# A transformer-like encoder layer on one core: the sums of the second MLP product's weights, made earlier and with GpSimd's own transfers

## The chip, the cores and the metric

The kernel runs on one core of a Trainium2 chip. A core has TensorE (matmuls; in the profile PE, with PEld for its weight loads), VectorE (DVE), ScalarE (ACT), GpSimd (POOL) and SyncE (SP). Each engine works through its own list of instructions in order and waits on semaphores for the others; transfers between memory and the on-chip buffer are issued as instructions of one engine's list and then run on 16 shared DMA engines. The metric is the device time of one execution in microseconds (us), the median of the runs shown. An engine's list that holds transfers is called its queue here.

## The reference

One encoder layer on 2048 tokens of width 1024, all in float32:

```
h   = RMSNorm(x);  z, xbc, dt, q, k, v = split(h @ W_in)
y_s = state-space heads(xbc, dt, z)          # forward and backward scan in chunks of 128
y_a = windowed attention(q, k, v)            # 16 heads, blocks of 128 with both neighbours
x   = x + RMSNorm(concat(y_s, y_a) @ W_out)
x   = x + RMSNorm(relu(RMSNorm(x) @ W_up)^2 @ W_down)
```

W_up is 1024 x 4096, W_down 4096 x 1024.

## The kernel before

Every array lies in tiles of 128 partitions by 512 columns. A float32 product is made of three matmuls in a rounded format: each operand is split into a high and a low part (`ws[:, 0]` and `ws[:, 1]` for weights), and high x high, high x low and low x high are summed in PSUM.

The main program works in this order: the input projection for the second half of the tokens (k and v, then eight q products), then for the first half (dt and v, k, q, then the convolution inputs and z), with attention blocks in between from the point where the second half's q, k, v are stored; the scan; the output projection; the two MLP products. TensorE's order is fixed by hand: `drive` advances the main generator and the side generators by an estimate of TensorE's time. The order on the other engines comes from the compiler's scheduler, which may put an instruction well ahead of the place where the program writes it, as soon as its inputs and buffers allow it.

**Weights of the input projection.** `wchunk` (L215 to L226) loads a tile `wr` from SyncE's queue, makes the high part with one GpSimd instruction (L222) and the low part with another (L225). There are four `ws` buffers of which a product uses two, so a product's weights are made while the one before it runs. `fill_h` and `split_slot` (L205) make the low parts of the normed input `h`, every second one on GpSimd; L342 and L343 split the weights of dt and v there.

**The MLP products** follow a fast algorithm for 2 x 2 blocks with 7 products for 8 (numbered 1 to 7 in the code), in two halves `hf` and groups `p` of seven steps of 12 matmuls. Its operands are sums of blocks. For the first product, `up_weights` makes the sums of W_up's blocks as it goes (L964, L969, L970), `up_input` and `up_input1` those of the input; the latter reads the second half's copies `dxo` from memory (L199 `stg`, L1012, L1013). Results go out by `dop` stores (L1079). For the second product, `down_weights` reads the sums of W_down's blocks from the array `dws` in memory, which `sums` fills.

**`sums`** (L1145) is a side generator, started in the first half of the first MLP product after group 3. It does 20 jobs, one after the other: four for the second half of x (load four tiles L1158, scale them on VectorE L1167, four operations on GpSimd L1169 to L1172, seven stores L1185 to `dxo`), then sixteen for W_down (load four tiles L1160, four additions or subtractions on GpSimd L1179, four stores L1187 to `dws`). Its tiles `sum` come from a set of four buffers (`nt`) that the norms use too. All its transfers are in SyncE's queue.

Of the kernel before, what the change touches and what calls it, by code (L numbers as in the profile page):

```python
# [38 lines left out]
class Layer:  # L39
# [73 lines left out]
    def drive(self, main):  # L113
        cond, mt = None, 0.0
        alive = True
        while alive or self.sides:
            s = next((s for s in self.sides if s[1] <= self.t and self.ready(s[2])), None)
            if s is not None:
                self.step_side(s)
            elif alive and mt <= self.t and self.ready(cond):  # L120
                cond, mt = next(main, self), self.t
                if cond is self:
                    alive, cond = False, None
                elif isinstance(cond, (int, float)):
                    mt, cond = self.t + cond, None
            else:
                c = [s[1] for s in self.sides if self.ready(s[2])]
                if alive and self.ready(cond):
                    c.append(mt)
                assert c, "stuck"  # L130
                self.t = max(self.t, min(c))
# [490 lines left out]
    def ssd_fwd(self, pool):  # L622
# [52 lines left out]
        def gate(c, g, y, sz, sums):  # L675
            pt = self.ps("pst")
            for i in range(4):
                self.tr(pt[:, i * P:(i + 1) * P], y[:, i * P:(i + 1) * P])
            nc.vector.tensor_mul(sz, sz, pt.rearrange("p (j t) -> p j t", j=4))
            nc.sync.dma_start(self.d_g[4 * g:4 * g + 4, :, c * P:(c + 1) * P].rearrange("j p t -> p j t"), sz)  # L680
            sq = pool.tile([P, 4, P], F32, tag="yt", name="gsq", bufs=2)
            nc.scalar.activation(sq, sz, AF.Square)
            s = pool.tile([P, P], F32, tag="gsum", name="gsum")
            nc.vector.reduce_sum(s, sq.rearrange("p j t -> p t j"), axis=mybir.AxisListType.X)
            if g:
                nc.vector.tensor_add(s, s, sums[c])
                nc.sync.dma_start(self.d_gs[:, c * P:(c + 1) * P], s)
                self.flags.add(f"ssd{c}")
            sums[c] = s
# [20 lines left out]
        for u in range(2 * NCH):  # L710
            c, g = u // 2, u % 2
            t0, pace = self.t, "ssd_pace2" if "att" in self.flags else "ssd_pace"
            if g == 0 and c < NCH - 1:
                ldn = self.ssd_load(pool, c + 1)
            if last:
                yield self.until(f"z{last[0] // 8}")
                sz = load_z(*last[:2])
            y = pool.tile([P, 512], F32, tag="y", name="y")
            yield from off(c, g, ld, prep, pb, y)
            nxt = prep  # L720
            if g and c < NCH - 1:
                if c + 1 < NCH - 1:
                    pb = load_pb(c + 1)
                yield K["ssd_p"]
                nxt = self.ssd_prep(pool, c + 1 == NCH - 1, *ldn)
            yield max(K["ssd_y"], t0 + K[pace] * K["ssd_f1"] - self.t)
            yield from diag(g, Es, ld[0], y)
            if last:
                gate(*last, sz, sums)
            yield max(K["ssd_y"], t0 + K[pace] * K["ssd_f2"] - self.t)  # L730
            if u < 2 * NCH - 1:
                Es = yield from expo((u + 1) % 2, *nxt[:3])
            last = (c, g, y)
            if g and c < NCH - 1:
                ld, prep = ldn, nxt
            yield max(K["ssd_y"], t0 + K[pace] - self.t)
        sz = load_z(*last[:2])
        yield 4
        gate(*last, sz, sums)


# [400 lines left out]

        self.pend.append(fn)

    def sums(self):  # L1145


        nc = self.nc
        vec = self.vec["norm_mlp_pre"]

        def load(job):
            a = {}
            for i in range(2):
                for k in range(2):
                    t = a[f"{i + 1}{k + 1}"] = self.nt("sum")
                    if len(job) == 1:
                        kt = 4 * i + job[0]
                        nc.sync.dma_start(t, self.d_x2[kt, :, self.tok(1, k)])  # L1158
                    else:
                        nc.sync.dma_start(t.rearrange("p (k c) -> p k c", k=4),  # L1160
                                          self.a["w_down"][2 * job[1] + i, 2 * job[0] + k])
            return a

        def x_sums(i, a):
            for y in ("11", "12", "22", "21"):
                kt = 4 * int(y[0]) - 4 + i
                nc.vector.tensor_scalar(a[y], a[y], vec[:, kt:kt + 1], None, ALU.mult)  # L1167
            t1, t2, t4 = self.ld(name="t1"), self.gl("t2"), self.ld(name="t4")
            nc.gpsimd.tensor_sub(t1, a["12"], a["11"])  # L1169
            nc.gpsimd.tensor_sub(t2, a["22"], t1)  # L1170
            nc.gpsimd.tensor_sub(a["12"], a["22"], a["12"])
            nc.gpsimd.tensor_sub(t4, a["21"], t2)  # L1172
            return {1: a["11"], 3: a["22"], 2: a["21"], 5: t1, 6: t2, 7: a["12"], 4: t4}

        def w_sums(qt, p, a):
            r = {}
            for m, fn, x, y, o in ((5, "tensor_add", "21", "22", "21"), (6, "tensor_sub", "21", "11", "11"),
                                   (7, "tensor_sub", "22", "11", "22"), (3, "tensor_sub", "12", "11", "12")):
                getattr(nc.gpsimd, fn)(a[o], a[x], a[y])  # L1179
                r[m] = a[o]  # L1180
            return r

        def store(m, job, a):
            if len(job) == 1:
                nc.sync.dma_start(self.d_xo[m - 1, job[0]], a)  # L1185
            else:
                nc.sync.dma_start(self.d_ws[(5, 6, 7, 3).index(m), job[0], job[1]], a)  # L1187
        jobs = [(i,) for i in range(4)] + [(qt, p) for qt in range(4) for p in range(4)]
        for n, job in enumerate(jobs):
            a = load(job)  # L1190
            yield 10
            r = (x_sums if len(job) == 1 else w_sums)(*job, a)
            yield 8
            for m, t in r.items():
                store(m, job, t)
            if n == 3:
                self.flags.add("xo")
            elif n > 3 and job[1] == 3:
                self.flags.add(f"sum{job[0]}")
            yield 5  # L1200

# [205 lines left out]
    def main(self):  # L1407
        nc, a, tc = self.nc, self.a, self.tc
# [50 lines left out]
        yield from self.dtvk(pp, 0, h, w)  # L1459
        yield from self.proj_q(pp, 0, h)  # L1460
        self.flags.add("qkv0")
        for c, j in self.p1a():
            yield from (self.proj_xbc(pp, 0, h, j) if c == "x" else self.proj_z(0, h, j))

# [74 lines left out]
        for hf in range(2):  # L1539
            for p in range(16):  # L1540
                if (hf, p) == (1, 15):
                    ws = itertools.chain(ws, self.down_weights())
                if p == 8:
                    self.side(self.r2(hf))
                if p == 14:
                    self.side(self.down_input() if hf else self.up_input1(B[1]))
                yield from self.up(hf, p, B[hf], wsa)
                if hf == 0 and p == 3:
                    yield self.until("x2_10", "x2_11")
                    s3.close()  # L1550
                    self.side(self.sums())
        self.worder = [("w_down", j, (6, 7)) for j in range(8)]
        while self.pend:
            self.pend.pop(0)()
# [108 lines left out]
```

## Time and profile before

| | us |
|---|---|
| median of 3 runs | 3213.89 |
| lowest and highest | 3203.62, 3218.38 |
| the profiled execution | 3205.63 |
| its span, first to last instruction | 3203.8 |

The profile's page shows one execution: busy time of each engine, the DMA queues, the chain of work that ended last. The trace behind it can be asked for a stretch: what an engine did in order of time (a timeline; in brackets the idle time before an instruction and what ended it), who waited for whom, and busy times and granted clock by stretch. TensorE's clock has two levels, 1.2 and 2.4 GHz; a granted clock of 1.00 is the upper one all the time.

### The profile page before, as it was taken

Reading aid. Unit: us, or ns where it says so; the run is one execution under the profiler, and the core shown is the slowest. Engines: PE = TensorE matmul, PEld = TensorE weight load, DVE = VectorE, ACT = ScalarE, POOL = GpSimd, SP = SyncE. Lnnn points to the kernel's source line nnn. Section 1 sums busy time; section 2 is a strip of 40 time slices with the busy share of each in tenths; the row PEclk is TensorE's granted clock in tenths of the full one; section 3 lists DMA queues with packets and bytes.
Section 4 is the critical chain, followed back from the end, with each engine's and each line's share of the span. In section 5 each row is a group of like instructions: output and inputs, shape, how many; then the busy total and the mean of one; then the engine's idle time right before and its main releaser. Section 6 shows DMA issues by size and latency. Waiting matters only on the chain. (4 is left out here: it accounts for less than half of the span.)

```text
span 3203.8 us, 41029 instructions
## 1 busy us (share of the span) xinstructions
PE 2949.0 (92%) x13560; PEld 2358.2 (74%) x13560; DVE 2196.2 (69%) x3671; ACT 1554.0 (49%) x2886; POOL 903.7 (28%) x743
## 2 busy tenths in 40 slices
PE   7989999989999899898897878998998999998996
PEld 6778887878886576576575657776887888877886
DVE  7355555547756778867868867677767567776765
ACT  4234566567765545322223354656565644454432
POOL 4242222112224344555545522141203000020001
PEclk9999999999999999899898989999999999999998
DMA  6767544465567755556436458778647565557633
GB/s 228 238 205 198 155 130 119 122 203 156 138 192 241 238 143 163 164 181 187 119 101 221 165 189 274 243 257 279 239 165 271 193 207 192 189 188 222 229 98 97
DMA packets 430213, 603.87 MB, mean 188 GB/s; under 512 B 35632, under 2 KB 203568, under 8 KB 430000
## 3 DMA queue, kind: packets, MB, share of 16 engines
q1 hardware_dynamic: 395376, 565.58, 57.0%
q10 hardware_dynamic: 34624, 35.66, 3.2%
q8 instruction: 108, 1.77, 0.2%
q14 instruction: 105, 0.86, 0.1%
HBM read 399.11 MB, written 201.99 MB: 188 GB/s over the span
## 5 line engine op out<-in xcount | busy, mean ns | idle before, releaser
L90 PE MATMUL psg<-h,ws 128*128 128x512 f32 x1920 | 486.6, 400 | 19.7 <-ACT z L474 17.9
L90 PEld LDWEIGHTS psg<-h,ws 128*128 128x128 f32 x1920 | 356.9, 190 | 93.4 <-issue 18.6
L88 PE MATMUL psmx<-b,ws 128*128 128x512 f32 x1152 | 297.0, 409 | 46.8 <-ACT c L1120 20.5
L222 POOL TENSOR_SCALAR ws<-wr 128x512 fp32r<-128x512 f32 x184 | 126.2, 686 | 755.9 <-PE psg L90 617.4
L88 PEld LDWEIGHTS psmx<-b,ws 128*128 128x128 f32 x1152 | 226.6, 198 | 102.3 <-ACT c L1120 22.4
L225 POOL TENSOR_TENSOR ws<-wr,ws 128x512 fp32r<-128x512 f32 x184 | 249.4, 1356 | 14.8
L90 PE MATMUL psg<-hr,ws 128*128 128x512 f32 x960 | 248.7, 400 | 4.0 <-DMA hr<-dh 3.3
L781 DVE CUSTOM_DVE_ANT_0 p<-psqk,pack,sinks 128x384 f32<-128x384 f32 (+1 forms) x256 | 151.9, 596 | 138.2 <-PE psqk L90 137.5
L90 PE MATMUL psg<-ga,ws 128*128 128x512 f32 x768 | 208.7, 424 | 28.9 <-DVE mix L897 14.2
L88 PE MATMUL psx<-ff,ws 128*128 128x512 f32 x1008 | 231.6, 390 | 0.0
L88 PEld LDWEIGHTS psx<-ff,ws 128*128 128x128 f32 x1008 | 189.2, 188 | 40.0 <-issue 0.5
L90 PE MATMUL psg<-ya,ws 128*128 128x512 f32 x768 | 213.0, 418 | 3.5 <-DVE ya L205 3.3
L969 ACT CAST ws<-wd 128x512 fp32r<-128x512 f32 x196 | 121.4, 622 | 177.6 <-PE psx L88 75.7
L90 PEld LDWEIGHTS psg<-ga,ws 128*128 128x128 f32 x768 | 149.4, 199 | 77.6 <-issue 13.6
L90 PEld LDWEIGHTS psg<-hr,ws 128*128 128x128 f32 x960 | 176.0, 189 | 40.8 <-DMA hr<-dh 6.1
L1179 POOL TENSOR_TENSOR sum<-sum 128x512 f32<-128x512 f32 x64 | 97.8, 1538 | 326.6 <-DMA sum<-w_down_dram 182.2
L90 PEld LDWEIGHTS psg<-ya,ws 128*128 128x128 f32 x768 | 142.0, 193 | 44.9 <-issue 15.1
L792 ACT ACTIVATE p<-p,m 128x384 f32<-128x384 f32 (+1 forms) x256 | 150.9, 591 | 37.4 <-DVE m L787 37.2
L90 PE MATMUL psy<-ff,ws 128*128 128x512 f32 x672 | 159.2, 394 | 7.2 <-DVE facc L1288 6.0
L210 ACT CAST pt<-pspt 128x512 fp32r<-128x512 f32 x184 | 107.0, 583 | 118.8 <-PE pspt L94 104.8
L970 DVE TENSOR_TENSOR ws<-wd,ws 128x512 fp32r<-128x512 f32 x196 | 137.7, 703 | 31.4 <-ACT ws L969 31.1
L211 DVE TENSOR_TENSOR pt<-pspt,pt 128x512 fp32r<-128x512 f32 x184 | 125.4, 683 | 49.2 <-ACT pt L210 48.8
(250 smaller groups left out, 6279.1 us busy)
## 6 DMA issues: line engine op xcount, KB each, us to landing
stg<-dop SPq DMA_DIRECT2D x196, 256.0 KB, 3.6
wu<-w_up_dram SPq DMA_DIRECT2D x128, 256.0 KB, 3.7
wr<-w_in_dram SPq DMA_DIRECT2D x120, 256.0 KB, 2.8
dop<-c SPq DMA_DIRECT2D x112, 256.0 KB, 3.4
wd<-dws SPq DMA_DIRECT2D x56, 512.0 KB, 4.2
k<-dk SPq DMA_DIRECT2D x56, 384.0 KB, 4.8
dop<-t SPq DMA_DIRECT2D x84, 256.0 KB, 3.5
wd<-w_down_dram SPq DMA_DIRECT2D x40, 512.0 KB, 4.7
```

Of the source, the lines that this page charges most:

```text
L88: self.nc.tensor.matmul(out, lhsT, rhs, start=False, stop=stop, skip_group_check=True)
L90: self.nc.tensor.matmul(out, lhsT, rhs, start=start, stop=stop)
L210: self.nc.scalar.copy(hi, src)
L211: self.nc.vector.tensor_sub(lo, src, hi.bitcast(F32))
L222: self.nc.gpsimd.tensor_scalar(w[:, 0], raw, 1.0, 0.0, ALU.mult, ALU.add)
L225: eng.tensor_sub(w[:, 1], raw, w[:, 0].bitcast(F32))
L781: nc.vector.tensor_tensor_reduce(out=p[:, :W], in0=ps[:, :W], in1=bias, scale=1.0, scalar=self.sinks[:, hd:hd + 1], op0=ALU.add, op1=ALU.m ...
L792: nc.scalar.activation(p4[r][:, :W], p4[r][:, :W], AF.Exp, bias=m[:, 0, r:r + 1], scale=float(np.float32(SLOPES[hd])), accum_out=m[:, 2, r ...
L969: self.nc.scalar.copy(w[:, 0], x)
L970: self.eng("wlo").tensor_sub(w[:, 1], x, w[:, 0].bitcast(F32))
L1179: getattr(nc.gpsimd, fn)(a[o], a[x], a[y])
```

## The change

The sixteen jobs for W_down become a side generator of their own, started after the q product of the first half, where the convolution inputs and z begin; the four jobs for x stay under the first MLP product. All transfers of `sums`, those for x too, are issued by GpSimd.

```diff
-    def sums(self):
+    def sums(self, jobs):
...
-                        nc.sync.dma_start(t, self.d_x2[kt, :, self.tok(1, k)])
+                        nc.gpsimd.dma_start(t, self.d_x2[kt, :, self.tok(1, k)])
                     else:
-                        nc.sync.dma_start(t.rearrange("p (k c) -> p k c", k=4),
+                        nc.gpsimd.dma_start(t.rearrange("p (k c) -> p k c", k=4),
                                           self.a["w_down"][2 * job[1] + i, 2 * job[0] + k])
...
             if len(job) == 1:
-                nc.sync.dma_start(self.d_xo[m - 1, job[0]], a)
+                nc.gpsimd.dma_start(self.d_xo[m - 1, job[0]], a)
             else:
-                nc.sync.dma_start(self.d_ws[(5, 6, 7, 3).index(m), job[0], job[1]], a)
-        jobs = [(i,) for i in range(4)] + [(qt, p) for qt in range(4) for p in range(4)]
+                nc.gpsimd.dma_start(self.d_ws[(5, 6, 7, 3).index(m), job[0], job[1]], a)
...
         self.flags.add("qkv0")
+        self.side(self.sums([(qt, p) for qt in range(4) for p in range(4)]))
         for c, j in self.p1a():
...
                     s3.close()
-                    self.side(self.sums())
+                    self.side(self.sums([(i,) for i in range(4)]))
```

In the built program the sums stand on GpSimd earlier than the text of the program says. The first place is under the last q products of the second half. Before, GpSimd's list has only weight steps there (the number behind a name is the buffer's; `ws_1132` and `ws_1137` are one product's two weight tiles):

```order
L222 TENSOR_SCALAR ws_1065<-wr_1063 128x512
L225 TENSOR_TENSOR ws_1065<-wr_1063,ws_1065 128x512
L222 TENSOR_SCALAR ws_1132<-wr_1130 128x512
L225 TENSOR_TENSOR ws_1132<-wr_1130,ws_1132 128x512
L222 TENSOR_SCALAR ws_1137<-wr_1135 128x512
L225 TENSOR_TENSOR ws_1137<-wr_1135,ws_1137 128x512
```

With the change the same piece of GpSimd's list reads:

```order
L222 TENSOR_SCALAR ws_1065<-wr_1063 128x512
L225 TENSOR_TENSOR ws_1065<-wr_1063,ws_1065 128x512
L1160 DMA sum_3300<-w_down_dram 128x512
L1160 DMA sum_3302<-w_down_dram 128x512
L1160 DMA sum_3304<-w_down_dram 128x512
L1160 DMA sum_3306<-w_down_dram 128x512
L1179 TENSOR_TENSOR sum_3304<-sum_3304,sum_3306 128x512
L1179 TENSOR_TENSOR sum_3300<-sum_3304,sum_3300 128x512
L1187 DMA dws_93<-sum_3304 128x512
L222 TENSOR_SCALAR ws_1132<-wr_1130 128x512
L1179 TENSOR_TENSOR sum_3306<-sum_3306,sum_3300 128x512
L225 TENSOR_TENSOR ws_1132<-wr_1130,ws_1132 128x512
```

Four loads, three operations and a store of the first job now stand ahead of the low part of `ws_1132`.

The second place is on GpSimd too, where the weights of dt and v and the first parts of the first half's `h` are made. Before:

```order
L225 TENSOR_TENSOR ws<-wr,ws 128x512
L342 TENSOR_SCALAR dtvh<-dtvr 128x1152
L343 TENSOR_TENSOR dtvl<-dtvr,dtvh 128x1152
L342 TENSOR_SCALAR dtvh<-dtvr 128x1152
L343 TENSOR_TENSOR dtvl<-dtvr,dtvh 128x1152
L205 TENSOR_TENSOR h<-xin,h 128x512 x7
```

With the change, from the first L343 on:

```order
L343 TENSOR_TENSOR dtvl<-dtvr,dtvh 128x1152
L1179 TENSOR_TENSOR sum<-sum 128x512
L1187 DMA dws<-sum 128x512
L1179 TENSOR_TENSOR sum<-sum 128x512 x2
L1187 DMA dws<-sum 128x512
L342 TENSOR_SCALAR dtvh<-dtvr 128x1152
L1187 DMA dws<-sum 128x512
L343 TENSOR_TENSOR dtvl<-dtvr,dtvh 128x1152
L1187 DMA dws<-sum 128x512
L1160 DMA sum<-w_down_dram 128x512 x3
L205 TENSOR_TENSOR h<-xin,h 128x512
```

The fourth job ends between the two weight tiles, and the fifth job's loads stand ahead of the first `h`. In the same way jobs six to eight stand whole between the weights of the second k product and of the first q product, and nine to sixteen one to a product.

The third place is SyncE's list under the first MLP product, where the first copies `dxo` are loaded (`dop` are results' stores, `wu` loads of W_up). Before:

```order
L1160 DMA sum<-w_down_dram 128x512 x4
L1079 DMA dop<-c_18558 128x512
L982 DMA wu<-w_up_dram 128x512 x2
L1187 DMA dws<-sum 128x512
L1079 DMA dop<-c_18528 128x512
L199 DMA stg<-dxo 128x512 x2
```

With the change:

```order
L1079 DMA dop<-t_18746 128x512
L982 DMA wu<-w_up_dram 128x512 x2
L1079 DMA dop<-c_18766 128x512
L982 DMA wu<-w_up_dram 128x512 x2
L1079 DMA dop<-c_18740 128x512
L199 DMA stg<-dxo 128x512 x2
```

The loads and stores of sums are gone from SyncE's list; TensorE's list is the same in both.

## Rows read from the trace of the kernel before

**Rows 1.** The page, part 1: busy us (share of the span) xinstructions.
```profile
PE 2949.0 (92%) x13560; PEld 2358.2 (74%) x13560; DVE 2196.2 (69%) x3671; ACT 1554.0 (49%) x2886; POOL 903.7 (28%) x743
```
**Rows 2.** Stretches: us, PE, PEld, DVE, ACT, POOL busy (x), PEclk, DMA share, GB/s.
```profile
2160.00:2240.00 80.00, 66.52 (x263) 51.63 (x264) 59.07 (x86) 48.27 (x87) 12.90 (x9) 0.91 0.84 279
2240.00:2320.00 80.00, 80.00 (x354) 66.26 (x353) 60.99 (x77) 45.03 (x76) 23.58 (x15) 1.00 0.69 240
...
2046.00:2466.00 420.00, 393.27 (x1689) 319.75 (x1687) 304.52 (x408) 239.70 (x406) 97.82 (x64) 0.98 0.70 242
134.00:332.00 198.00, 185.16 (x946) 158.46 (x945) 104.50 (x229) 74.52 (x179) 67.92 (x62) 0.97 0.72 207
```
**Rows 3.** Timeline of SyncE's queue, 2148 to 2169: start us, us, what.
```profile
2153.18 2.75 SPq L1160 DMA_DIRECT2D sum<-w_down_dram  x4
...
2156.45 0.94 SPq L982 DMA_DIRECT2D wu<-w_up_dram  x2
2161.57 0.33 SPq L1187 DMA_DIRECT2D dws<-sum  x1
...
2162.43 0.94 SPq L199 DMA_DIRECT2D stg<-dxo  x2
```
**Rows 4.** Timeline of TensorE: four of its stalls in the first MLP product.
```profile
1994.83 4.60 PE L88 MATMUL psmx<-b,ws 128*128 128x512 f32 x12 [2.86 <-ACT c L1120]
...
2069.59 4.39 PE L88 MATMUL psmx<-b,ws 128*128 128x512 f32 x12 [3.09 <-DVE c L1123]
...
2168.33 5.26 PE L88 MATMUL psmy<-b,ws 128*128 128x512 f32 x12 [9.83 <-ACT c L1120]
...
2466.51 4.69 PE L88 MATMUL psmx<-b,ws 128*128 128x512 f32 x12 [8.47 <-DVE c L1123]
```
**Rows 5.** Waits of SyncE's queue, 2046 to 2466: us in total, times, longest.
```profile
SPq L1187 <- POOL sum L1179: 68.9, 46, 3.2
```
**Rows 6.** Timeline of ScalarE at 2063 and 2460, of SyncE's queue at 2441.
```profile
2063.60 1.28 ACT L282 ACT_TABLE_LOAD   x1 [5.00 <-DMA dws<-sum]
...
2441.57 5.42 SPq L1187 DMA_DIRECT2D dws<-sum  x4
...
2460.71 0.62 ACT L1246 CAST ff<-stg 128x512 fp32r<-128x512 f32 x1 [9.69 <-DMA stg<-dop]
```
**Rows 7.** The page, part 5: GpSimd's two weight steps; busy, mean ns, idle before.
```profile
L222 POOL TENSOR_SCALAR ws<-wr 128x512 fp32r<-128x512 f32 x184 | 126.2, 686 | 755.9 <-PE psg L90 617.4 <-DMA wr<-w_in_dram 96.1 <-PE pspt L94 24.1
...
L225 POOL TENSOR_TENSOR ws<-wr,ws 128x512 fp32r<-128x512 f32 x184 | 249.4, 1356 | 14.8
```
**Rows 8.** Tile sum: stores' issue; page, part 6: landing; tile wr, 130 to 340.
```profile
L1187 SPq DMA_DIRECT2D dws<-sum x64: 319/326/1042, 2061.5 to 2465.2; - x64
...
dws<-sum SPq DMA_DIRECT2D x64, 256.0 KB, 2.1
...
DMA to landing us min/median/max: 2.6/4.2/6.5
```
**Rows 9.** Timeline of GpSimd, pieces from 138 to 322.
```profile
138.59 0.62 POOL L222 TENSOR_SCALAR ws<-wr 128x512 fp32r<-128x512 f32 x1 [4.17 <-DMA wr<-w_in_dram]
...
190.49 1.64 POOL L205 TENSOR_TENSOR h<-xin,h 128x512 fp32r<-128x512 f32 x1 [1.33 <-ACT h L204]
...
206.88 1.05 POOL L222 TENSOR_SCALAR ws<-wr 128x512 fp32r<-128x512 f32 x1
...
236.14 0.62 POOL L222 TENSOR_SCALAR ws<-wr 128x512 fp32r<-128x512 f32 x1 [23.32 <-PE psg L90]
...
306.60 0.62 POOL L222 TENSOR_SCALAR ws<-wr 128x512 fp32r<-128x512 f32 x1 [2.47 <-PE psg L90]
...
321.27 0.62 POOL L222 TENSOR_SCALAR ws<-wr 128x512 fp32r<-128x512 f32 x1 [2.36 <-PE psg L90]
```
**Rows 10.** Timeline of TensorE, 128 to 204.
```profile
134.01 42.75 PE L90 MATMUL psg<-h,ws 128*128 128x512 f32 x186
186.73 0.58 PE L90 MATMUL psdtv<-dtvh,h 128*128 128x288 f32 x1 [9.97 <-issue]
```
**Rows 11.** Timeline of VectorE, 134.9 to 139: the norm's last step.
```profile
137.62 0.69 DVE L288 SCALAR_TENSOR_TENSOR rb<-rs_t,rb 128x512 f32<-128x512 f32 x1
```

More of the change, by code (lines that the diff above doesn't have):

```diff
@@ L1195, in sums @@
                 store(m, job, t)
-            if n == 3:
-                self.flags.add("xo")
-            elif n > 3 and job[1] == 3:
+            if len(job) == 1:
+                if n == 3:
+                    self.flags.add("xo")
+            elif job[1] == 3:
                 self.flags.add(f"sum{job[0]}")
```

## The prediction

> **What bounds the kernel now.** I read the page's busy shares first: TensorE is busy 92% of the span, no other engine over 74% [rows 1]. TensorE's order is written out and the change doesn't touch it, so time moves only where TensorE waits. I therefore cut the span into stretches and looked at two: the first MLP product, from which the 64 weight sums leave, and the input projection with the first attention blocks, where the new GpSimd order puts them.
>
> In the first product a full stretch of 80 us holds 354 matmuls (0.226 us each, 2.72 for a step of 12), the stretch 2160 to 2240 only 263, at a granted clock of 0.91 [rows 2]. The timelines show why. SyncE is through with its weight loads at 2157.4 and then stands before a store of a sum; GpSimd, which makes the sum, waits for loads that SyncE itself issued only from 2153.2 to 2155.9; the store leaves at 2161.6, and behind it the load of `stg` that ScalarE waits for [rows 3]. ScalarE, held, evicts late, and TensorE stands 9.83 us; its next 12 matmuls take 5.26 us, not 2.72 [rows 4]. Over the stretch SyncE waits 68.9 us at these stores for GpSimd [rows 5].
>
> In the input projection the reader is to see that GpSimd makes the weights (L222 and L225) that TensorE multiplies with next, with little in hand early on and one product in hand later.
>
> **The gain.** 128 transfers (64 loads, 64 stores) leave SyncE's queue, and 64 subtractions leave GpSimd between 2046 and 2466. I count the TensorE stalls whose chain goes through them:
> - 2168.33: 9.83 + (5.26 - 2.72) = 12.4 us [rows 4].
> - 2466.51: 8.47 + (4.69 - 2.72) = 10.4 us [rows 4]. SyncE stood 5.42 us at four sum stores from 2441.6, the `stg` loads behind them came late, and ScalarE waited 9.69 us for one [rows 6].
> - 2069.59: 3.09 + 1.67 = 4.8 us [rows 4]: a norm's table load on ScalarE waited 5.00 us for a sum's store to free its buffer [rows 6].
>
> Together 28 us. I leave two stalls in place: the one at 1994.83 (2.86 + 1.88 = 4.7 us [rows 4]), since the 16 sums over x stay there and VectorE still waits for their loads, and what else is missing in 2160 to 2240: 91 matmuls are 20.6 us, of which the stall above takes 10.8 after 2160, so 9.8 hang on copies that are loaded after each other. With both the gain is 42; if SyncE's next wait takes over part of it, 20. The 44 transfers of the x sums cost GpSimd nothing that counts: it was idle three quarters of that stretch (97.8 of 420 us busy [rows 2]).
>
> **The cost.** The printed order puts all 16 jobs of sums among GpSimd's weight steps between the pair that begins at 138.59 and the step at 321.27 in the trace of before [rows 9]. GpSimd works its list in order, so a sum that waits for its load holds every weight step behind it, and TensorE, which waited only for other things there, waits for the weights. One job is:
> - 4 two-input operations at 1.36 us [rows 7], the same kind and size as L225: 5.4.
> - 8 issues. No GpSimd issue stands in the trace. Nearest below: SyncE's issue of such a store, 0.33 us [rows 8]. Nearest above: a two-input GpSimd operation on the tile, 1.36. I take 0.69, the cheapest GpSimd operation on a tile of this size (L222 [rows 7]), since it lies between and is GpSimd's own: 5.5.
> - One wait for a load, 4.2 us (the median landing of the weight loads in this very stretch), and one for the store before it to free the buffer, 2.1 [rows 8].
>
> That is 17.2 us a job; with a product's two weight steps (4.1) 21.3. By order:
> - Jobs 1 to 3, under the last three q products of the second half. 42.75 us hold 186 matmuls, so a product of 48 takes 11.0, and the one fed by the pair at 138.59 begins 33 us before 176.76, at 143.7 [rows 9, 10]. The sum's buffers come free at 138.3, when a norm's last step ends [rows 11]; the last load is issued at 139.0 and lands at 143.2; two subtractions, one issue, L222, a subtraction and L225 end at 150.0: 6 late. Each further job is 21.3 against 11.0, less some 1.5 of waiting that weight steps cover: 2 x 9 = 18. Sum 24.
> - Jobs 4 and half of 5, among the dt/v weights and the first four `h` parts, for which TensorE stood idle 9.97 us already [rows 10]: 1.5 x 17.2 = 26, less about 6 of GpSimd's idle time there (four or five waits like the 1.33 [rows 9]) and, as I estimate, 4 in hand: 16.
> - The rest of 5 to 8, three jobs' worth before the weights of q's first product: 52, less the 23.3 us of idle time before 236.14 [rows 9] and, again an estimate, 10 in hand: 18 or so.
> - Jobs 9 to 16, one to a product. Products follow each other at 14.7 (306.60 to 321.27 [rows 9]); a job with its steps is 21.3, less 2.5 covered: 4.1 late each, 33.
>
> Together 91 us. Each 0.1 us of issue is 12.8 us over 128 issues: 45 at 0.33, 177 at 1.36. A second floor comes from the transfers: 128 x 0.262 MB = 33.6 MB, at 242 GB/s for a share of 0.70 in the first product, is 97 us of all engines; 134 to 332 uses 0.72 of 198 us = 143 already [rows 2]. 240 us don't fit into 198: at least 42 late, whatever an issue costs.
>
> One page bears on the price of an issue. The Trainium skill, "DMA: Bandwidth & Descriptors", section "Latency and other measured facts", gives about 1 us to the first byte for GpSimd's software path and about 0.6 for SyncE's; no row here shows either. With 1 us for an issue the 91 would be 131.
>
> **The sum.** 91 - 28 = 63. The profiled execution takes 3205.6 us, 8.3 below the median of the runs; so 3269 there and **3277 us** as a median. Bounds: 45 - 42 = +3 (3217) and 177 - 20 = +157 (3371).
>
> **Rivals.** A measurement of this kernel tells about 0.5% (16 us) from no change.
> - *Faster, by hiding:* an issue costs GpSimd nothing (8 x 0.69 = 5.5 a job falls away), the jobs fit into its idle time from the third group on, 17 late remains (8 in the first group, 8 in the second, 1 in the third), and all 42 come back: -25, 3189. For it: GpSimd is idle 130 of 198 us there [rows 2]. Against: the floor of 42 by transfers, and loads that wait within the list. It decides below some 0.3 us an issue. Chance 0.09.
> - *No change:* the floor of 42 alone, against a gain of 42: 3214. For it: both are read from rows. Against: it needs every bound at its best. Chance 0.13.
> - *Much slower:* GpSimd's issue is held up by VectorE, which is busy 104.5 of the 198 us [rows 2]; at 1.36 an issue 177 late, +149, 3363. For it: L222 took 1.05 us at 206.88 where it takes 0.62 elsewhere [rows 9]. Against: L225 spreads little here. Chance 0.21. The Trainium skill, "SBUF — State Buffer", section "SBUF: two separate sides", has such a rule: while VectorE runs certain operations GpSimd can't write a transfer's descriptors, and the transfer waits; no run here shows it yet.
>
> **Numbers.** The forecast (an issue between 0.33 and 1.02, halfway from 0.69 to 1.36: 45 - 42 = +3 to 133 - 20 = +113) has 0.57. Faster 0.09; within 0.5% 0.14, the no-change case and a sliver of the forecast's lower end; slower 0.77. The range goes from 3205 to 3350: it leaves out the faster case and about half of the much slower one.
>
> **What would show it.** In the changed profile: L1187 gone from SyncE's waits, the three stalls gone; between 134 and some 420 us L222, L225 and `h` preceded by sums on GpSimd, and TensorE waiting for GpSimd's `ws` and `h` for tens of us where it now waits for nothing of the kind; the first late weight at about 144, by 6 us, 24 by the end of the q products, 40 at the dt/v product, 91 when the last sum is stored. It is wrong if GpSimd's issues take far from 0.69, if landings move away from 4.2, or if the first product finds other stalls.

## The result, and the profile after

| | before | after |
|---|---|---|
| median, us | 3209.63 (4 runs) | 3293.35 (4 runs) |
| lowest to highest | 3203.62 to 3218.38 | 3283.46 to 3298.92 |
| profiled execution | 3205.63 | 3289.85 |

The ratio is 1.0252, with a 95% interval of 1.0229 to 1.0275: the change makes the kernel slower, by 84 us in the profiled execution. The forecast was 3277, the range 3205 to 3350.

The page of the changed kernel, part 1 and the new queue of part 3, beside [rows 1]:

```profile
PE 2979.8 (91%) x13560; PEld 2375.8 (72%) x13560; DVE 2185.4 (66%) x3671; ACT 1553.6 (47%) x2886; POOL 979.6 (30%) x915
...
q0 software_dynamic: 13760, 45.10, 4.0%
```

TensorE runs the same 13560 matmuls, but they take 30.8 us longer in sum; GpSimd has its own queue of 45 MB. Since the matmuls stand in the same order in both kernels, the start of the same matmul in the two traces tells where the time went (differences worked out before rounding):

| matmul no. | starts before, us | after, us | later by |
|---|---|---|---|
| 516 (under the last q products of the second half) | 128.9 | 128.4 | -0.4 |
| 700 | 172.5 | 201.2 | 28.7 |
| 1000 | 236.1 | 279.2 | 43.0 |
| 1200 | 275.6 | 350.7 | 75.1 |
| 1640 (behind the last sum's store) | 365.8 | 473.3 | 107.5 |
| 8200 (first MLP product) | 1924.0 | 2033.4 | 109.4 |
| 8400 | 1979.2 | 2096.0 | 116.8 |
| 9000 | 2126.2 | 2234.9 | 108.8 |
| 9300 | 2210.7 | 2303.9 | 93.2 |
| 10600 (second MLP product) | 2523.2 | 2604.3 | 81.1 |
| 13559 | 3188.2 | 3269.1 | 81.0 |

So 108 us are lost in one stretch, 28 come back in another, and elsewhere the sum hardly moves (1.9 us between matmuls 1640 and 8200). The two stretches by the same matmuls; first the kernel before (columns as in [rows 2]), input projection and first MLP product:

```profile
128.90:365.80 236.90, 223.10 (x1126) 189.44 (x1125) 120.95 (x270) 90.96 (x217) 80.76 (x75) 0.97 0.72 204
...
1924.00:2523.20 599.20, 562.38 (x2402) 457.42 (x2402) 424.05 (x580) 334.13 (x568) 129.99 (x84) 0.97 0.68 235
```

and the changed kernel:

```profile
128.40:473.30 344.90, 253.49 (x1126) 204.83 (x1126) 146.16 (x270) 90.88 (x217) 229.52 (x267) 0.85 0.75 238
...
2033.40:2604.30 570.90, 555.22 (x2402) 453.22 (x2401) 387.82 (x580) 335.02 (x569) 53.91 (x64) 0.99 0.54 188
```

The reader is to split the 108: the same 1126 matmuls are busy 253.5 us instead of 223.1, and the rest of the stretch, TensorE idle, is 91.4 instead of 13.8. So **78 us are waiting and 30 us are slower matmuls**, at a granted clock of 0.85 instead of 0.97. TensorE's timeline in the stretch (its larger stalls; there was none for GpSimd over 0.6 us before):

```profile
148.46 1.22 PE L90 MATMUL psg<-h,ws 128*128 128x512 f32 x2 [5.13 <-POOL ws L222]
...
173.43 1.22 PE L90 MATMUL psg<-h,ws 128*128 128x512 f32 x2 [9.59 <-POOL ws L222]
...
215.29 0.58 PE L90 MATMUL psdtv<-dtvh,h 128*128 128x288 f32 x1 [9.84 <-issue]
...
298.89 3.43 PE L90 MATMUL psg<-h,ws 128*128 128x512 f32 x6 [9.50 <-POOL ws L222]
...
336.57 3.43 PE L90 MATMUL psg<-h,ws 128*128 128x512 f32 x6 [13.30 <-POOL ws L222]
```

The product at 336.57 shows both parts in one row: 13.30 us of idle time, then 0.57 us for each matmul where 0.23 is usual. GpSimd's timeline at the first of these stalls:

```profile
133.56 1.27 POOL L1160 DMA_DIRECT2D sum<-w_down_dram  x2
136.36 0.54 POOL L1160 DMA_DIRECT2D sum<-w_down_dram  x1 [1.53 <-DVE rs_t L286]
137.81 0.54 POOL L1160 DMA_DIRECT2D sum<-w_down_dram  x1 [0.91 <-DVE rb L288]
144.65 2.59 POOL L1179 TENSOR_TENSOR sum<-sum 128x512 f32<-128x512 f32 x2 [6.30 <-DMA sum<-w_down_dram]
147.18 0.56 POOL L1187 DMA_DIRECT2D dws<-sum  x1
147.77 0.63 POOL L222 TENSOR_SCALAR ws<-wr 128x512 fp32r<-128x512 f32 x1
```

GpSimd stands 6.30 us for the load that it issued itself, and only then makes the weight (L222) for which TensorE has been waiting. Over the whole stretch (us in total, times, longest) TensorE's waits for GpSimd were these before:

```profile
PE psg L90 <- POOL ws L225: 0.6, 1, 0.6
PE psg L90 <- POOL ws L222: 0.3, 1, 0.3
```

With the change, TensorE's and then GpSimd's:

```profile
PE psg L90 <- POOL ws L222: 46.7, 9, 13.3
...
PE psg L90 <- POOL ws L225: 9.9, 11, 1.7
...
PE psdtv L90 <- POOL h L205: 5.4, 3, 2.8
...
POOL sum L1179 <- DMA sum<-w_down_dram: 58.1, 15, 6.5
POOL sum L1160 <- DMA dws<-sum: 25.4, 24, 3.2
```

Those of TensorE are 62 us. Of the others 10.4 us, in three waits, are for VectorE's `qst`, where none stood before. I followed the longest: SyncE's load of the next raw weights had stood 7.4 us for a buffer that GpSimd had not emptied yet, the stores of `qst` (`dq`) left behind it, ScalarE stood for these, and TensorE behind it:

```profile
447.09 0.69 ACT L461 ACTIVATE qst<-psg,pack 128x512 fp32r<-128x512 f32 x1 [7.42 <-DMA dq<-qst]
```
```profile
448.62 2.93 PE L90 MATMUL psg<-h,ws 128*128 128x512 f32 x6 [5.58 <-DVE qst L462]
```

So GpSimd's list held TensorE by SyncE's list as well. And the prices of what was added, from the tile `sum` (ns, least, median and most):

```profile
L1160 POOL DMA_DIRECT2D sum<-w_down_dram x64: 536/541/1023, 133.6 to 426.3; - x64
L1179 POOL TENSOR_TENSOR sum<-sum x64: 1254/1286/1867, 144.6 to 435.7; 128x512 f32<-128x512 f32 x64
L1187 POOL DMA_DIRECT2D dws<-sum x64: 539/562/598, 147.2 to 440.0; - x64
```

### The profile page after: what moved, and what is told of

Read it like the earlier page. It is cut to its first block, busy times and chain, and to the rows that moved or that the text cites. A ratio compares the mean times of both kernels' runs of the same rounds, so it can differ in the third digit from the quotient of the medians.

```text
span 3288.1 us, 40939 instructions
## 1 busy us (share of the span) xinstructions
PE 2979.8 (91%) x13560; PEld 2375.8 (72%) x13560; DVE 2185.4 (66%) x3671; ACT 1553.6 (47%) x2886; POOL 979.6 (30%) x915
## 5 line engine op out<-in xcount | busy, mean ns | idle before, releaser
L90 PE MATMUL psg<-h,ws 128*128 128x512 f32 x1920 | 510.7, 412 | 86.1 <-POOL ws L222 46.7
L90 PEld LDWEIGHTS psg<-h,ws 128*128 128x128 f32 x1920 | 367.0, 197 | 173.2 <-POOL ws L222 50.9
L222 POOL TENSOR_SCALAR ws<-wr 128x512 fp32r<-128x512 f32 x184 | 126.5, 688 | 635.4 <-PE psg L90 555.4
L913 POOL TENSOR_TENSOR facs<-facs,sq 128x512 f32<-128x512 f32 x14 | 19.2, 1373 | 743.8 <-ACT sq L912 743.8
L970 DVE TENSOR_TENSOR ws<-wd,ws 128x512 fp32r<-128x512 f32 x196 | 138.2, 706 | 30.6 <-ACT ws L969 30.1
```

Of the source, the lines that this page charges most:

```text
L90: self.nc.tensor.matmul(out, lhsT, rhs, start=start, stop=stop)
L222: self.nc.gpsimd.tensor_scalar(w[:, 0], raw, 1.0, 0.0, ALU.mult, ALU.add)
L913: (eng or nc.vector).tensor_add(acc[b], acc[b], q)
L970: self.eng("wlo").tensor_sub(w[:, 1], x, w[:, 0].bitcast(F32))
```

## The experiments

Each run is compared with runs of the kernel before on the same chip. "Late by" is worked out as in the table above, from the starts of the same matmuls; the input projection is counted up to matmul 4400 (951 us before), the first MLP product from 8200 to 10600 (599.2 us before).

### What made the 28 us in the first product

**All sums back at the old place, with GpSimd's queue** (e1):

```diff
-        self.side(self.sums([(qt, p) for qt in range(4) for p in range(4)]))
...
-                    self.side(self.sums([(i,) for i in range(4)]))
+                    self.side(self.sums([(i,) for i in range(4)] + [(qt, p) for qt in range(4) for p in range(4)]))
```

> All sums back at their old place under the first MLP product, all their transfers issued by GpSimd. Theory (the whole loss comes from the place on GpSimd's list under the input projection, the whole gain from SyncE's list being freed): no TensorE wait for ws from GpSimd between 130 and 440 us, matmul stretch of the input projection as before, and the 28 us of the first product come back, so a ratio to before of about 0.991 (some 3182 us where before takes 3210). Rival A (the gain comes from the 33.6 MB that leave the first product, not from the queue): the stalls of 9.8 and 8.5 us stay in some form, ratio 0.996 to 1.000. Rival B (GpSimd's list is too slow for sums even there): the sums are late for the second product, ratio over 1.0.

Measured: 1.0171 (1.0142 to 1.0199). The input projection is as before (2 us late at matmul 4400), the first product takes 644.9 us, 46 more. Rival B came true, by a mechanism that I hadn't in mind. One row of GpSimd and one of TensorE:

```profile
2427.64 0.54 POOL L1160 DMA_DIRECT2D sum<-w_down_dram  x1 [136.84 <-DVE ws L970]
```
```profile
2516.09 4.96 PE L88 MATMUL psmx<-b,ws 128*128 128x512 f32 x12 [25.78 <-ACT c L1120]
```

A sum's load stood 136.84 us for a buffer of the set `nt`, which by then held raw weights of the second product (`wd`, L970) that were loaded early and used late; the sums behind it came late, and SyncE then stood 19.7 us at a load of the second product's raw weights for a buffer that a late sum still held, with the `stg` loads for which ScalarE waited behind it:

```profile
SPq L1218 <- DMA sum<-w_down_dram: 19.7, 1, 19.7
```

This explains less than half of the 46 us: matmuls 9400 to 10600, where the stall lies, lose 17.5, and matmuls 9000 to 9400 lose 18, whose cause stays open.

**The same, with `wd` asking for its buffers after the last sum** (e8; `lastsum` is the newest sum's tile):

```diff
                             for x in range(2):
+                                nc.gpsimd.tensor_scalar(raw[x][:, 0, :4], self.lastsum[:, :4], 1.0, 0.0, ALU.mult, ALU.add)
                                 nc.sync.dma_start(raw[x], self.a["w_down"][2 * (p + x), 0])
```

> All sums at the old place with GpSimd's queue again, but the two buffers that the second product's first raw weights take from the sums' set are now asked for after the last sum (four columns of each are overwritten from it first). In the first try of this place GpSimd stood 137 us for such a buffer and the sums came late. Theory A (SyncE's list was the stall's cause, so the queue alone brings the gain): ratio 0.991 to 0.994. Theory B (the sums' traffic and operations in that stretch are the cause, whichever queue issues): ratio 0.998 to 1.002. Theory C (GpSimd's jobs, 17 us each in order, are too slow for that place even so): sums late for the second product, ratio over 1.004.

Measured: 1.0144 (1.0116 to 1.0173). The edit missed its aim: a sum's load still stood 139.1 us for such a buffer, and TensorE 27.05 us. The ratio is theory C's, but the hold is that of e1, so the run says nothing on theory A. Of the 48 us lost in the first product some 20 lie at this stall; 18 others lie between matmuls 9000 and 9400, and what causes them stays open.

**The kernel before without the 64 operations** (e5): their transfers stay in SyncE's queue.

```diff
-                getattr(nc.gpsimd, fn)(a[o], a[x], a[y])
                 r[m] = a[o]
```

> The kernel before, with the 64 additions and subtractions of the weight sums left out (loaded blocks are stored as they are; the second MLP product multiplies other weights); their transfers stay in SyncE's queue under the first product. What makes the 28 us that the change gains there? Theory A (SyncE stands before a store that waits for GpSimd, 68.9 us of such waits): the store now waits for the load alone, so some of it goes: ratio 0.994 to 0.997. Theory B (GpSimd's operations slow VectorE's there: its steps from buffer to buffer took 773 to 789 ns under the sums and 689 without): nearly all goes, ratio 0.990 to 0.993. Theory C (the 128 transfers in SyncE's queue and their 33.6 MB): ratio 0.998 to 1.000.

Measured: 0.9928 (0.9906 to 0.9950). The first product takes 575.8 us, 23 less, with all 128 transfers still in SyncE's queue: theory B's number. C falls. A's number is exceeded, though the interval reaches into A's range (0.994 to 0.997), and SyncE's waits for GpSimd at the stores are gone here too: the run shows that the operations cost this time, not by which way.

**The kernel before with these operations on VectorE** (e10), one word:

```diff
-                getattr(nc.gpsimd, fn)(a[o], a[x], a[y])
+                getattr(nc.vector, fn)(a[o], a[x], a[y])
```

> The kernel before with one word changed: the 64 additions and subtractions of the weight sums run on VectorE, at their old place and with SyncE's transfers. Without them the ratio was 0.9928. VectorE takes some 0.69 us for one and is freed of GpSimd's slowing there. Theory A (the slowing was the larger part, and SyncE's store waits for a shorter step): ratio 0.992 to 0.996. Theory B (VectorE, 305 of 420 us busy there and in TensorE's path, is held by waits for the sums' loads in its own list): ratio 0.999 or more.

Measured: 0.9913 (0.9899 to 0.9927), 3185.55 us; the first product takes 573.4. Groups of VectorE between 2046 and 2540 (count, busy us, mean ns, idle before) in the kernel before:

```profile
L970 DVE TENSOR_TENSOR ws<-wc,ws 128x512 fp32r<-128x512 f32 x91 | 69.0, 762 | 14.1 <-ACT ws L969 14.1
...
L1086 DVE TENSOR_TENSOR t<-c,t 128x512 f32<-128x512 f32 x20 | 20.6, 1032 | 0.5
...
L1123 DVE TENSOR_TENSOR c<-c,psmx 128x512 f32<-128x512 f32 x23 | 15.8, 685 | 22.3 <-PE psmx L88 22.3
```

and with the sums on VectorE:

```profile
L970 DVE TENSOR_TENSOR ws<-wc,ws 128x512 fp32r<-128x512 f32 x92 | 62.9, 687 | 11.3 <-ACT ws L969 11.0
...
L1086 DVE TENSOR_TENSOR t<-c,t 128x512 f32<-128x512 f32 x20 | 13.7, 686 | 0.2
...
L1123 DVE TENSOR_TENSOR c<-c,psmx 128x512 f32<-128x512 f32 x24 | 16.4, 684 | 15.6 <-PE psmx L88 15.6
...
L1179 DVE TENSOR_TENSOR sum<-sum 128x512 f32<-128x512 f32 x64 | 43.6, 687 | 15.4 <-DMA sum<-w_down_dram 14.0 <-DMA dop<-t 0.9
```

VectorE's steps with both inputs in the on-chip buffer took 762 and 1032 ns in the mean while GpSimd made sums, and 687 and 686 without; those with one input in PSUM (L1123) took 685 and 684. The means mix two kinds of steps. Of the 20 of L1086 in the kernel before, the 13 that met none of GpSimd's two-input operations took 694 ns at most, and each of the 7 that overlapped one took 1665 to 1670; the nine steps of L1123 that overlapped one took 689 at most. VectorE is busy 424.1 us of that product before and 419.8 with 64 operations more: it does the sums in the time in which GpSimd had held it up. The Trainium skill, "SBUF — State Buffer", section "Who interferes with whom", has this rule: a VectorE instruction that reads two operands from the buffer contends with a GpSimd instruction that reads there, one with at most a single such operand doesn't, as long as it is outside VectorE's two-port fast modes. These rows agree with both halves of it. A single operand alone is no protection in this kernel: the attention's scaling of `p` (L800, L801 in e4), which reads one tile and a column of factors, took 943 ns in the mean between 440 and 850 us in e4, whose GpSimd makes sums there, and 518 before. In the same two runs SyncE's waits at the sums' stores for the sum fell too (68.9 us before, 39.2 here), so how the 26 us divide between the two effects, VectorE's freed steps and SyncE's shorter waits, isn't settled.

### What made the 108 us in the input projection

**New place, transfers from SyncE** (e2):

```diff
-                        nc.gpsimd.dma_start(t.rearrange("p (k c) -> p k c", k=4),
+                        nc.sync.dma_start(t.rearrange("p (k c) -> p k c", k=4),
...
-                nc.gpsimd.dma_start(self.d_ws[(5, 6, 7, 3).index(m), job[0], job[1]], a)
+                nc.sync.dma_start(self.d_ws[(5, 6, 7, 3).index(m), job[0], job[1]], a)
```

and likewise for the sums of x.

> Sums of the weights at the new place, all transfers of sums issued by SyncE as before. Theory (what holds GpSimd's list is the issues, 0.54 us each, and the waits for loads to land and stores to free the buffers; the 64 subtractions alone fit): TensorE's waits for GpSimd's ws between 130 and 440 us fall from 57 us to under 15, ratio to before 0.992 to 0.999 (3185 to 3207 us). Rival A (the transfers' 33.6 MB under the input projection are what costs, at least 42 us): ratio 1.004 or more. Rival B (SyncE's list, held at stores that wait for GpSimd, makes the weight loads late instead): TensorE's waits move to ws behind DMA wr, ratio 1.003 to 1.02.

Measured: 1.0049 (1.0031 to 1.0066). Up to matmul 1640 the kernel is only 2 us late, with DMA at a share of 0.78 there, and TensorE doesn't stand for GpSimd's weights as it did. But only 17 of the 64 loads fall into that stretch: the scheduler spreads these jobs to 579 us, so the run says little of the traffic of all sixteen. Between matmuls 1640 and 2400 it loses 49. SyncE's waits from 368 to 576 us, and one of TensorE's stalls with what stands ahead of it on SyncE's list and on ScalarE:

```profile
SPq L1187 <- POOL sum L1179: 53.3, 35, 3.3
...
SPq L1187 <- DMA sum<-w_down_dram: 28.9, 10, 5.3
```
```profile
496.04 3.81 SPq L1187 DMA_DIRECT2D dws<-sum  x3
...
503.03 0.38 SPq L492 DMA_DIRECT2D dxh<-craw  x1
```
```profile
506.35 0.59 ACT L210 CAST pt<-pspt 128x512 fp32r<-128x512 f32 x1 [11.13 <-DMA dxh<-craw]
```
```profile
515.24 2.90 PE L90 MATMUL psg<-h,ws 128*128 128x512 f32 x6 [12.28 <-ACT z L474]
```

That is rival B in kind, with loads and stores of the attention and the convolution held instead of the weights'. The first product takes 569.9 us: the gain is there with the x sums on either queue.

**New place, loads from SyncE, stores from GpSimd** (e11; x sums on SyncE):

```diff
-                        nc.gpsimd.dma_start(t.rearrange("p (k c) -> p k c", k=4),
+                        nc.sync.dma_start(t.rearrange("p (k c) -> p k c", k=4),
```

> The change with the weight sums' loads issued by SyncE, and only their 64 stores by GpSimd, which makes the sums; x sums on SyncE. So no list waits for a load to land except GpSimd's operations, and SyncE stands at no store. Theory A (what costs is an engine's list waiting for transfers: the change 108 us late on GpSimd's list, the version with all on SyncE 49 late at stores): under 25 us late by 950 us, ratio 0.993 to 0.999. Theory B (GpSimd's operations slowing the attention's VectorE steps cost some 20 us wherever they stand in that stretch): 20 to 30 late, ratio 0.998 to 1.002. Theory C (the loads' waits for buffers hold SyncE's list all the same): 40 or more late, ratio over 1.003.

Measured: 1.0146 (1.0127 to 1.0164), 74 us late at matmul 4400. My theory A is refuted in this form, theory C holds: the loads now stand on SyncE's list for the buffers that the stores still read.

```profile
SPq L1160 <- DMA dws<-sum: 65.5, 22, 8.7
```

In e2 and here GpSimd's operations also stretch short VectorE steps of the attention (128 x 4 elements: L787 took 740 ns in the mean in e2, L794 1035 here, where 156 and 216 stood before). How much of the 49 and the 74 that is, theory B here, these two runs don't separate.

**The change without the 64 operations** (e3; the second product's weights differ):

> The change with the 64 additions and subtractions of the weight sums left out: the loaded blocks are stored as they are, so the second MLP product multiplies other weights; all 128 transfers stay on GpSimd's list at the new place. Theory (GpSimd's list in order; a job falls from 17 to some 11 us of list): worked through in the new order with 0.54 us an issue, 4.3 a landing and 2.5 a store, TensorE waits only some 9 us, with the lower clock 10 to 20; minus the gain of 28 this is a ratio of 0.994 to 0.998 (3190 to 3203 us). Rival A (the transfers' bandwidth: 240 us of all engines' time in 198): 42 us or more late, ratio at least 1.004. Rival B (an issue is held by VectorE's work and costs more the denser they stand): issues' mean over 0.7 us, ratio over 1.004.

Measured: 1.0147 (1.0130 to 1.0163), 72 us late at matmul 4400, where I expected 10 to 20. The same 1126 matmuls take 306.0 us, 50 of the 69 more being idle time. Issues took 0.54 us, so rival B falls. Theory and rival A this run can't separate: without operations the scheduler put the same transfers between fewer weight steps (all within 136 to 338 us), DMA had a share of 0.86, the transfers of `sum` landed after 5.4 us in the median (the loads alone after 5.6), and GpSimd stood nearly as long for loads and for freed buffers as with the operations (us, times):

```profile
  DMA sum<-w_down_dram: 51.4, 32
  DMA dws<-sum: 24.0, 21
...
DMA to landing us min/median/max: 2.3/5.4/8.7
```

By this run the operations are the smaller part of the 108, some 38; the transfers on the list that feeds TensorE, with their issues, waits and traffic together, are the larger. Since they stood denser here, the split isn't exact.

**The sums held back to where the program starts them** (e4): each load first has four columns of its buffer overwritten from the newest weight tile, so that it can't stand ahead of that weight step.

```diff
+                        nc.gpsimd.tensor_scalar(t[:, :4], self.lastw[:, 1, 0, :4].bitcast(F32), 1.0, 0.0, ALU.mult, ALU.add)
                         nc.gpsimd.dma_start(t.rearrange("p (k c) -> p k c", k=4),
```

> The change, with the weight sums held back to where the program starts them: each of their loads first has four columns of its buffer overwritten from the newest weight tile, so that it can't go ahead of that weight step on GpSimd's list (64 small operations more). The jobs then stand under the convolution inputs and z, after the last q product, one job to one or two products of 17 us and more, with DMA at a share of 0.44 to 0.59 there before. Theory: one job (17 us) and two weight steps (4) are done before the product after the next begins, so TensorE waits under 5 us in all for GpSimd's ws; with the gain of 28 the ratio is 0.991 to 0.994 (3182 to 3191 us). Rival (a job costs about 4 us of TensorE's time wherever it stands on this list, as under the q products): 16 jobs, 64 us, ratio 1.01.

Measured: 0.9985 (0.9970 to 1.0000). TensorE hardly waits for GpSimd's weights any more, and the gain of 27 in the first product is there, but 22 us are lost before matmul 4400, at ScalarE's `z` that stands behind the attention. VectorE's timeline at one such place, and GpSimd's:

```profile
510.28 0.16 DVE L789 TENSOR_TENSOR m<-m,hp 128x4 f32<-128x4 f32 x1
514.41 2.91 DVE L795 TENSOR_TENSOR m<-m 128x4 f32<-128x4 f32 x1 [3.96 <-ACT p L793]
517.36 0.18 DVE L796 RECIPROCAL m<-m 128x4 f32<-128x4 f32 x1
```
```profile
511.59 2.68 POOL L1181 TENSOR_TENSOR sum<-sum 128x512 f32<-128x512 f32 x2 [5.06 <-DMA sum<-w_down_dram]
514.21 0.56 POOL L1189 DMA_DIRECT2D dws<-sum  x1
514.79 2.50 POOL L1181 TENSOR_TENSOR sum<-sum 128x512 f32<-128x512 f32 x2
```

An operation on 128 x 4 elements, 0.16 us for its neighbour L789, took 2.91 and ended when GpSimd's two subtractions did; by this trace it began 0.4 us before them, and spans on GpSimd are rough, so the row alone is a hint. The means say the same: L795 took 567 ns between 440 and 850 us, 286 before (L794 there), and the scaling of `p` 943, 518 before.

**That kernel without the operations** (e6), and **with them on VectorE** (e7), there held until the next weight step by two small VectorE operations that multiply by a one made behind that step on GpSimd; the pause behind a job's loads is 20 there, not 10 (not shown):

```diff
+            one = self.tp.tile([P, 1], F32, tag="one", name="one", bufs=2)
+            nc.gpsimd.tensor_scalar(one, self.lastw[:, 1, 0, :1].bitcast(F32), 0.0, 1.0, ALU.mult, ALU.add)
+            for y in ("22", "11"):
+                nc.vector.tensor_scalar(a[y][:, :4], a[y][:, :4], one, None, ALU.mult)
...
-                getattr(nc.gpsimd, fn)(a[o], a[x], a[y])
+                getattr(nc.vector, fn)(a[o], a[x], a[y])
```

> The held-back kernel (weight sums pinned to the weight steps under the convolution inputs and z, ratio 0.9985, 22 us lost there) with its 64 additions and subtractions left out; the same 128 transfers on GpSimd's list. Theory A (what costs 22 us there is GpSimd's operations slowing VectorE's, the attention's scaling of p took 921 ns there and 518 before): under 6 us lost, ratio 0.991 to 0.993. Theory B (the transfers delay the attention's loads): 15 to 22 us lost, ratio 0.996 to 0.999.

> The held-back kernel with the 64 additions and subtractions on VectorE (some 0.69 us each, where GpSimd takes 1.29), held until the next weight step so that VectorE doesn't wait for the loads; loads and stores stay on GpSimd's list. VectorE has 249 of 410 us busy there and gets 44 more. Theory A (GpSimd's operations slowing VectorE's are the cost): under 10 us lost of 22, ratio 0.991 to 0.995, the fastest kernel of the case. Theory B (the transfers, or VectorE as the attention's bound): 20 us or more lost, ratio 0.998 or more.

Measured: 0.9936 (0.9913 to 0.9960) and 0.9933 (0.9910 to 0.9957). At matmul 4400 the first is 7 us late, the second 2. Theory A in both: 16 to 20 of the 22 us came with the operations' place on GpSimd, and 33.6 MB of transfers cost little there. The places move a little with each edit (the last sum's store leaves at 829 us in e4, 803 in e6 and 971 in e7).

**The last one, with the x sums' transfers back on SyncE** (e9):

```diff
-                        nc.gpsimd.dma_start(t, self.d_x2[kt, :, self.tok(1, k)])
+                        nc.sync.dma_start(t, self.d_x2[kt, :, self.tok(1, k)])
...
-                nc.gpsimd.dma_start(self.d_xo[m - 1, job[0]], a)
+                nc.sync.dma_start(self.d_xo[m - 1, job[0]], a)
```

> The held-back kernel with its sums on VectorE (ratio 0.9933), with the transfers of the sums over x back in SyncE's queue; only those of the weights stay with GpSimd. In every kernel with the x sums on GpSimd's queue the 200 matmuls from some 1924 to 1979 us were 6 to 8 us later than in the kernel before, in the one with them on SyncE 0.8. Theory A (GpSimd's list makes the first x sums late): these 6 to 8 us go, ratio 0.990 to 0.992. Theory B (it is won back at the next stall anyway, as the stall of 4.8 us at 2069 was): no change against 0.9933 within its interval.

Measured: 0.9891 (0.9872 to 0.9909), 3178.72 us. Matmuls 8200 to 8400 take 56.0 us instead of 63.2: theory A at that place, but more than half of it is lost again later (matmuls 8400 to 10600 take 517.8 instead of 513.8), partly as theory B had it. Of the 7 us the product keeps 3, and the two profiled executions differ by 3 (3185.76 and 3188.74); the medians differ by 11, which the traces don't explain. This kernel and the one-word change e10 both beat the kernel before; their intervals overlap, so which of the two is faster isn't told.

## Why the prediction was right, and where it was not

**The mechanism was right.** TensorE's waits for GpSimd rose from under 1 us to 62 in the stretch, and the lateness grew much as the steps had it: the first late weight 6.4 us at 148.46 and 150.91 (forecast 6 at about 144), 28.6 at the beginning of dt/v's product (186.73 to 215.29; forecast 24), 43 at matmul 1000 (forecast 40), 108 at the end (forecast 91). That these come so close is in part luck: the forecasts are waiting alone, and of the measured lateness waiting is 21 at matmul 700, 30 at matmul 1000 and 78 at the end, the rest slower matmuls.

**The price of a job was too high.** An issue took 0.54 to 0.56 us, not 0.69: 128 times 0.14 is 18 us of lateness by the prediction's own rule. An operation took 1.29, not 1.36; the waits within the list were 58.1 and 25.4 us, 5.2 a job, where 6.3 stood. By the issue alone, waiting should have come out at 73 instead of 91; it was 78. With the operation and the waits too a job takes 14.8 us instead of 17.2, and sixteen times 2.4 less leaves some 52. So waiting came out 26 above what its own rule gives at the measured prices: 10.4 of them are the waits for `qst`, which the steps didn't have. For the rest the estimates of what lay in hand and of covered waits may have been too generous; that isn't shown.

**The largest step that failed is a missing term: the slower matmuls behind each stall.** On the side of the gain I had counted them (5.26 for 2.72 us, and so on); on the side of the cost I counted waiting alone. The granted clock fell from 0.97 to 0.85 and the same matmuls took 30 us more. Waiting 13 less and the matmuls 30 more than reckoned make the 17 us by which the cost was missed. The profiled execution was missed by 21 (3289.9 for 3269; the rest lies outside these stretches), the median by 16, since it stands 3.5 above that execution and not 8.3.

**The gain had the right size, 28.3 for 28, by luck, and the transfers' leaving SyncE's list isn't what it needs.** Matmuls 8400 to 10600 gained 35.6, and 8200 to 8400, at the x sums, lost 7.4, for which the sum had nothing. I gave the gain to SyncE's list. With SyncE's transfers left where they were, 23 to 26 us came from taking GpSimd's operations away or to VectorE (e5, e10). A kernel in which only SyncE's list is freed and nothing else happens I didn't get (e1, e8). The stalls that I left in place did not stay either: the one at 1994.83 went and another, 4.46 us, came some 10 steps of 12 matmuls earlier, while the x sums ran; of the copies' 9.8 us some 4 went and 6 stayed (the 262 matmuls behind the stall at 2168.33 took 71.5 us before and 65.2 now, where 59.2 would be full pace).

**"The x sums cost GpSimd nothing that counts" was wrong.** GpSimd was idle enough, but its waits within the list made the first copies late: 7.4 us between matmuls 8200 and 8400. Moving these transfers back was worth 7 us there and 3 over the whole product (e9 beside e7).

**The rivals.** The floor by transfers isn't seen to bind: in the changed kernel DMA's share of the stretch is 0.75, and e7 lost 2 us with all transfers on GpSimd's list, further on and over some 600 us. But no run put them all into 198 us without that list in TensorE's way: e2 had 17 of 64 loads there, and in e3, which was 70 late, DMA's share was 0.92 from 136 to 338. So the floor itself stays untested. Issues held up by VectorE fell: 541 ns in the median and 1023 at most of 64 loads, 562 and 598 of 64 stores, while VectorE was busy 146 of 345 us. The rule of the Trainium skill, "SBUF — State Buffer", section "SBUF: two separate sides", that VectorE can in certain operations hold up the writing of descriptors, thus shows no effect on an issue's time here. The microsecond to the first byte that the Trainium skill, "DMA: Bandwidth & Descriptors", section "Latency and other measured facts", gives for GpSimd's path would have made 131 us of waiting for 91, an estimate, if it were the list's time. The list's time is 0.54, and no run here shows the first byte by itself.

## What to carry to other kernels

An engine's idle share alone doesn't say whether a job fits on it: a job that waits for memory within an in-order list delays all that stands behind it, so first ask who waits for that list and how much it has in hand, and hold background work by a real dependency at a place where one step lies in hand. Count a stall at what it costs with the slower matmuls after it, on both sides of the sum. Before moving background work to another time, ask whom its engine holds up where it runs now: here one word, GpSimd's sums made on VectorE, brought most of the gain that the change was to bring, without its price.

## What the runs showed of the hardware that I had not expected

- A transfer's issue takes 0.54 to 0.56 us of GpSimd's list in the median (1.02 at most of 128), where SyncE's store took 0.33 [rows 8]; its loads of 256 KB landed 4.9 us after the issue in the median.
- GpSimd's two-input operations stretch those of VectorE that read both inputs from the buffer: on 128 x 512 from 692 ns to 1667 for each that overlaps one (L1086), 686 to 1032 in the mean of the group, and on 128 x 4 up to 2.91 us for 0.16. Those that read one input from PSUM keep their time (685 and 684 ns).
- A freed buffer is worth a look of its own: in e1 and e8 a background job stood 137 and 139 us for a buffer that a later stage's load had taken early.
